# Making the RWKV output gates of a half sequence in one stream of matrix products

## The chip, the cores and the metric

The program runs on one core of one Trainium2 chip. The metric is the time of one execution on the device in microseconds; three executions of the kernel before took 3402.66, 3409.33 and 3413.01 us (median 3409.33). The profiled execution is a fourth one.

## The reference

A two-layer decoder over 1024 positions with 1024 channels, batch 1, all in float32: layer 0 is an RWKV-7 time mixing and a squared-ReLU MLP, layer 1 a forgetting attention on a shared K/V and a second MLP. Each is preceded by an RMS norm with a shift and a scale made from a conditioning vector. The part that the change touches is the output gate `g` of the time mixing:

```python
xr, xw, xk, xv, xa, xg = (h + xx * mu[j] for j in range(6))   # xx: shifted token minus token
r = xr @ wr; k = xk @ wk; v = xv @ wv
g = jax.nn.sigmoid(xg @ g1) @ g2          # g1 (1024, 160), g2 (160, 1024)
y = wkv7_scan(rh, decay, kh, vh, -kk, kk * ah)      # 16 heads of 64, one step a token
y = group_norm(y) * ln_w + ln_b + bonus
return (y * g) @ wo
```

## The kernel before

Everything lies transposed: 128 channels of one of 8 blocks on the partitions, tokens along the free axis. The sequence is cut into two halves of 512 tokens. A large product (`proj`, L150) takes one 128x1024 weight block at a time: SP loads it into `wraw`, ACT rounds it to float32r into `wh` (L116), POOL makes the remainder `wl` (L117), and `mm3` (L120) adds three float32r passes of TensorE into one PSUM bank: wh x hh (L124), wh x hl (L126), wl x hh (L128). The inputs are split in the same way: ACT casts `hh` (L166), DVE subtracts `hl` (L167). `wraw`, `wh` and `wl` have two buffers each. Products on plain float32 operands, as the small ones of the recurrence, take two MATMUL instructions each in the trace.

`phase_rwkv` (L440) makes what layer 0 needs: `stream` (L581) computes r, k and v of a half and stores them in DRAM, its mixed inputs coming from `shift` (POOL, L658) and `mix` (DVE, L663). The conditioning vector's products are made on DVE (`mod`, L182), spread between these. `lora_g` (L564) computes sigmoid(xg @ g1): two float32 products per channel block (L573), one of 128 rows and one of 32, then Tanh on ACT (L577) and a multiply-add on POOL (L578). The 128 rows go to DRAM as `gad` (L579), the 32 stay in partitions 96 to 127 of `zt`.

`phase_wkv` (L667) is the recurrence, in 16 units of two channel blocks by 256 tokens. Units 0 to 7 are the first half, 8 to 15 the second. `early` and `late` prepare a unit, `chain` (L845) runs its four chunks of 64 tokens one after the other, with three steps each, and `gate` (L916) finishes it while the next unit's chain runs: the group norm (L923 to L928), the weights lnw and lnb (L935, L936), then the gate. For this it loads `gad` and the two blocks of g2 (L921, L933, L934), multiplies them with float32 products, 128 rows (L937) and 32 rows (L938) for each of the two channel blocks, and DVE multiplies y with the result in PSUM (L940).

The order is set in two layers. In the program, `units` (L955) gives each step of a chain a ration of `early` and `late`, of the last unit's `gate`, and of dense work from another generator (`beside`): the streams of the second half, then the output product wo and the MLP of the first half. A `yield` in that code is one piece of a ration. In the first half, `rest` (L534) runs `lora_g` beside the end of the r stream, before unit 0. On top of that, the tile framework schedules the instructions of each engine by a simulated timeline, and gives the chain's steps priority. Each engine then runs its own list in order.

## Time and profile before

| | |
|---|---|
| median of three executions | 3409.33 us |
| the profiled execution | 3409.55 us, its span 3407.8 us (1.75 us lie outside) |
| TensorE, matmul busy | 3212.7 us (94% of the span), mean granted clock 0.969 |
| DVE / ACT / POOL busy | 2092.3 / 1431.1 / 1368.4 us (61% / 42% / 40%) |
| start and end of the gates | first gate product at 394.71 us, last one at 1313.83 us |

A matmul's busy time is from its start to its modelled end, and neighbours overlap in the pipeline, so what a product costs TensorE is read from the start of one to the start of the next. "Idle before" is the time in which an engine had nothing running ahead of an instruction, with the instruction that ended the wait. The span divides for this change into the preparation of the first half (up to about 330 us), the 16 units (330 to 1320 us), and the rest, in which the layer's second half, the MLPs and the attention follow.

### The profile page before, as it was taken

How to read it: one execution, taken by the hardware profiler on the slowest of the kernel's cores; microseconds unless marked ns; L12 is line 12 of the kernel's file. 1: busy time of each engine (PE TensorE's matmuls, PEld its weight loads, DVE VectorE, ACT ScalarE, POOL GpSimd, SP SyncE). 2: the span in 40 equal slices, each digit the busy share in tenths (PEclk: the TensorE clock that was granted, in tenths of full speed). 3: DMA queues.
4: the chain of work that ended last, by engine and by line, in shares of the span. 5: the costliest groups of instructions: out<-in, count | busy, mean ns of one | idle time of the engine just before them, and what ended most of it. 6: DMA issues, size and time to landing. Idle time of an engine off the chain costs nothing. (4 is left out here: it accounts for less than half of the span.)

```text
span 3407.8 us, 50293 instructions
## 1 busy us (share of the span) xinstructions
PE 3212.7 (94%) x19108; PEld 2441.4 (72%) x19108; DVE 2092.3 (61%) x3239; ACT 1431.1 (42%) x2284; POOL 1368.4 (40%) x868
## 2 busy tenths in 40 slices
PE   4798999999999998899999999999999999999997
PEld 2466666666777776678878777777778888778886
DVE  7496765666656546377795433555577776455555
ACT  3632236433423223242242556667555454332323
POOL 3464333333433333454434432444433333554444
PEclk7899999899999999999999999999999999999999
DMA  7365344354333225345542233666544442232322
GB/s 270 104 231 154 94 123 139 119 151 143 100 91 106 88 75 177 124 130 173 184 137 95 82 134 115 208 200 182 174 128 138 143 134 95 91 105 99 99 96 84
DMA packets 294064, 452.88 MB, mean 133 GB/s; under 512 B 114720, under 2 KB 170432, under 8 KB 293824
## 3 DMA queue, kind: packets, MB, share of 16 engines
q1 hardware_dynamic: 293824, 449.68, 42.2%
q8 instruction: 151, 2.47, 0.3%
q14 instruction: 89, 0.73, 0.1%
HBM read 371.25 MB, written 78.32 MB: 132 GB/s over the span
## 5 line engine op out<-in xcount | busy, mean ns | idle before, releaser
L117 POOL TENSOR_TENSOR wl<-wraw,wh 128x1024 fp32r<-128x1024 f32 x385 | 951.4, 2472 | 1221.8 <-ACT wh L116 1164.2
L116 ACT CAST wh<-wraw 128x1024 fp32r<-128x1024 f32 x385 | 402.6, 1046 | 709.8 <-PE pk L126 298.2
L124 PE MATMUL pj<-hh,wh 128*128 128x512 f32 x1120 | 449.8, 409 | 9.2 <-ACT wh L116 2.2
L128 PE MATMUL pj<-hh,wl 128*128 128x512 f32 x1120 | 443.2, 401 | 6.0 <-POOL wl L117 6.0
L126 PE MATMUL pj<-hl,wh 128*128 128x512 f32 x1120 | 442.3, 400 | 0.0
L1040 DVE TENSOR_TENSOR mr<-mr 128x512 f32<-128x512 f32 x128 | 276.7, 2163 | 221.5 <-ACT mr L1039 221.3
L1010 DVE SCALAR_TENSOR_TENSOR x<-pj,G,x 128x512 f32<-128x512 f32 x304 | 223.8, 745 | 130.9 <-PE pj L128 129.6
L128 PE MATMUL pk<-hh,wl 128*128 128x512 f32 x688 | 273.5, 404 | 9.7 <-POOL wl L117 9.7
L124 PE MATMUL pk<-hh,wh 128*128 128x512 f32 x688 | 271.5, 400 | 9.7 <-ACT wh L116 6.7
L126 PE MATMUL pk<-hl,wh 128*128 128x512 f32 x688 | 269.4, 398 | 0.0
L124 PEld LDWEIGHTS pj<-hh,wh 128*128 128x128 f32 x1120 | 210.8, 189 | 64.8 <-issue 4.6
L128 PEld LDWEIGHTS pj<-hh,wl 128*128 128x128 f32 x1120 | 210.6, 188 | 59.8 <-POOL wl L117 8.4
L124 PE MATMUL pj<-mh,wh 128*128 128x512 f32 x564 | 237.2, 421 | 17.0 <-DVE x L1010 16.8
L126 PEld LDWEIGHTS pj<-hl,wh 128*128 128x128 f32 x1120 | 210.6, 188 | 47.2 <-issue 2.6
L166 ACT CAST mh<-mr 128x512 fp32r<-128x512 f32 x128 | 79.4, 620 | 372.6 <-DVE mr L1040 206.3
L126 PE MATMUL pj<-ml,wh 128*128 128x512 f32 x564 | 224.4, 398 | 0.0
L1010 DVE SCALAR_TENSOR_TENSOR x<-pk,G,x 128x512 f32<-128x512 f32 x240 | 173.6, 744 | 81.5 <-PE pk L128 81.5
L128 PE MATMUL pj<-mh,wl 128*128 128x512 f32 x564 | 218.6, 399 | 0.0
L182 DVE SCALAR_TENSOR_TENSOR modacc<-modw,cact,modacc 128x1024 f32<-128x1024 f32 x98 | 162.7, 1661 | 39.6 <-DMA modw<-in_modw_dram 26.1
L124 PE MATMUL pk<-mh,wh 128*128 128x512 f32 x460 | 181.4, 396 | 3.5 <-DVE x L1010 3.5
L126 PE MATMUL pk<-ml,wh 128*128 128x512 f32 x460 | 181.3, 394 | 0.0
L128 PE MATMUL pk<-mh,wl 128*128 128x512 f32 x460 | 167.1, 397 | 2.0 <-POOL wl L117 2.0
(333 smaller groups left out, 6502.3 us busy)
## 6 DMA issues: line engine op xcount, KB each, us to landing
wraw<-in_up_dram SPq DMA_DIRECT2D x128, 512.0 KB
wraw<-in_down_dram SPq DMA_DIRECT2D x128, 512.0 KB
modw<-in_modw_dram SPq DMA_DIRECT2D x96, 512.0 KB
wraw<-in_wqg_dram SPq DMA_DIRECT2D x32, 512.0 KB
wraw<-in_wk_dram SPq DMA_DIRECT2D x24, 512.0 KB
wraw<-in_wv_dram SPq DMA_DIRECT2D x24, 512.0 KB
x<-in_xT_dram SPq DMA_DIRECT2D x32, 256.0 KB
wraw<-in_wr_dram SPq DMA_DIRECT2D x16, 512.0 KB
```

The source lines that it names most:

```text
L116: nc.scalar.copy(out=wh, in_=raw)
L117: self.weng.tensor_tensor(out=wl, in0=raw, in1=wh.bitcast(F32), op=ALU.subtract)
L124: mm(out=p, lhsT=wh, rhs=hh[k], start=first, stop=False)
L126: mm(out=p, lhsT=wh, rhs=hl[k], start=False, stop=False)
L128: mm(out=p, lhsT=wl, rhs=hh[k], start=False, stop=last)
L166: self.nc.scalar.copy(out=out_h, in_=src)
L182: nc.vector.scalar_tensor_tensor(out=acc, in0=w, scalar=ck, in1=acc, op0=ALU.mult, op1=ALU.add)
L1010: self.nc.vector.scalar_tensor_tensor(out=x[j][m], in0=ps, scalar=gain[:, m:m + 1], in1=x[j][m], op0=ALU.mult, op1=ALU.add)
L1040: nc.vector.tensor_tensor(out=r, in0=r, in1=r, op=ALU.mult)
```

## The change

`lora_g` now goes on to the gate itself. The 128 rows of sigmoid(xg @ g1) are split into `gh` and `gl`, the 32 last rows into three blocks of one tile `gr`: the rounded rows in partitions 0 to 31 and again in 64 to 95, the remainder in 32 to 63. g2's first 128 rows are loaded as a weight block with `load_w`, its last 32 three times into one block `wr`, whose third copy becomes the remainder. Then, for each of the 8 channel blocks, three passes of `mm3` and one pass with `wr` and `gr` (96 rows) give g; ACT evicts it and SP stores it in DRAM (`gd`). `gate` loads the 128x512 block of g that its unit needs and multiplies it with y on POOL. The bank of `pms` that held the float32 gate products, the loads of g2 and `gad`, and the DVE multiplication go. `gate` has one yield less, `lora_g` eight more.

```diff
--- before.py
+++ after.py
@@ -292,7 +292,7 @@
             self.Fd = dt("Fd", [NH, 2, T])
             self.Ld = dt("Ld", [2 * KT, 128, 8, HD])
             self.T16d = dt("T16d", [2 * KT, 2, 64, 256])
-            self.gad = dt("gad", [128, T])
+            self.gd = dt("gd", [KT, 128, T])
 
             self.tp = self.pool(es, "tmp", 4)
             self.wp = self.pool(es, "wring", 3)
@@ -303,7 +303,7 @@
 
             er = es.enter_context(ExitStack())
             zp = self.pool(er, "zp")
-            self.zt = zp.tile([128, T], F32, name="zt")
+            self.zt = zp.tile([65, T], F32, name="zt")
             self.sv = zp.tile([128, KT, HD], F32, name="sv")
             self.pe = self.pool(er, "pe", space=PSUM)
             el = es.enter_context(ExitStack())
@@ -529,10 +529,10 @@
             yield from self.lora_wa(h, 1, lw, al)
             for i in (1, 2, 0):
                 yield from self.stream(h, 1, i, xj, ev, al)
-            yield from self.lora_g(h, 1, lw)
+            yield from self.lora_g(h, 1, lw, xj, ev)
 
         def rest():
-            for _ in self.both(self.lora_g(h, 0, lw), r, 3):
+            for _ in self.both(self.lora_g(h, 0, lw, xj, ev), r, 3):
                 self.take(m, self.NMD)
                 yield
             self.drain(m)
@@ -561,22 +561,44 @@
         S.activation(out=self.zt[0:64, s], in_=ps[0:64], func=AF.Tanh)
         S.copy(out=al[:, s], in_=ps[64:128])
 
-    def lora_g(self, h, j, lw):
-
-        nc, S = self.nc, self.nc.scalar
+    def lora_g(self, h, j, lw, xj, ev):
+
+
+        nc, S, V, G = self.nc, self.nc.scalar, self.nc.vector, self.nc.gpsimd
         s = slice(j * HT, (j + 1) * HT)
         ps = [self.bank() for _ in range(2)]
         for k in range(KT):
             w = lw(("g1",), k)
             xg = self.mix(h[j][k], self.shift(h[j][k]), 5, k)
-            for p, o, n in ((ps[0], 0, 128), (ps[1][96:128], 128, 32)):
+            for p, o, n in ((ps[0], 0, 128), (ps[1][0:32], 128, 32)):
                 nc.tensor.matmul(out=p, lhsT=w[:, o:o + n], rhs=xg, start=k == 0, stop=k == KT - 1)
                 yield
         g = self.t()
-        for a, p in ((g, ps[0]), (self.zt[96:128, s], ps[1][96:128])):
-            S.activation(out=a, in_=p, func=AF.Tanh, scale=0.5)
-            nc.gpsimd.tensor_scalar(out=a, in0=a, scalar1=0.5, scalar2=0.5, op0=ALU.mult, op1=ALU.add)
-        nc.sync.dma_start(out=self.gad[:, s], in_=g)
+        gh, gl = (xj.tile([128, HT], F32R, name=n, tag=n) for n in ("xh", "xl"))
+        S.activation(out=g, in_=ps[0], func=AF.Tanh, scale=0.5)
+        G.tensor_scalar(out=g, in0=g, scalar1=0.5, scalar2=0.5, op0=ALU.mult, op1=ALU.add)
+        self.split(gh, gl, g)
+        r = self.t()
+        gr = xj.tile([128, HT], F32R, name="xh", tag="xh")
+        S.activation(out=r[0:32], in_=ps[1][0:32], func=AF.Tanh, scale=0.5)
+        G.tensor_scalar(out=r[0:32], in0=r[0:32], scalar1=0.5, scalar2=0.5, op0=ALU.mult, op1=ALU.add)
+        S.copy(out=gr[0:32], in_=r[0:32])
+        S.copy(out=gr[64:96], in_=r[0:32])
+        V.tensor_tensor(out=gr[32:64], in0=r[0:32], in1=gr[0:32].bitcast(F32), op=ALU.subtract)
+        wh, wl = self.load_w(self.ap["g2"][:, 0:128].rearrange("m k n -> k m n"))
+        raw, wr = (self.wp.tile([128, KT, 128], d, name=n, tag=n, bufs=b) for n, d, b in (("wraw", F32, self.NW[0]), ("wh", F32R, self.NW[1])))
+        for i in range(3):
+            nc.sync.dma_start(out=raw[i * 32:(i + 1) * 32], in_=self.ap["g2"][:, 128:160].rearrange("m k n -> k m n"))
+        S.copy(out=wr[0:96], in_=raw[0:96])
+        self.weng.tensor_tensor(out=wr[64:96], in0=raw[64:96], in1=wr[64:96].bitcast(F32), op=ALU.subtract)
+        for m in range(KT):
+            p = self.bank()
+            self.mm3([p], wh[:, m], wl[:, m], [(j, [gh], [gl])], 0, True, False)
+            nc.tensor.matmul(out=p, lhsT=wr[0:96, m], rhs=gr[0:96], start=False, stop=True)
+            yield
+            o = ev.tile([128, HT], F32, name="e0", tag="e0")
+            S.copy(out=o, in_=p)
+            nc.sync.dma_start(out=self.gd[m][:, s], in_=o)
 
     def stream(self, h, half, which, xj, ev, al, lead=2):
 
@@ -917,8 +939,8 @@
 
             j, p, ts = where(u)
             y, bv, rs = w["y"], self.t(), self.t()
-            ga = lng("ga", [128, 256], 1)
-            nc.sync.dma_start(out=ga, in_=self.gad[:, ts])
+            g = lng("g", [128, W], 1)
+            nc.sync.dma_start(out=two(g), in_=pair(self.gd, p, ts))
             nc.sync.dma_start(out=two(bv), in_=pair(self.bvd, p, ts))
             S.activation(out=rs, in_=y, func=AF.Square)
             ps = self.small()
@@ -926,18 +948,12 @@
             yield
             S.activation(out=rs, in_=ps, func=AF.Ln, bias=self.gneps)
             S.activation(out=rs, in_=rs, func=AF.Exp, scale=-0.5)
-            ps = self.small()
             for q in range(2):
                 c = slice(q * 256, (q + 1) * 256)
-                g2 = lng("g2", [128, 2, 128], 1)
-                nc.sync.dma_start(out=g2[:, 0], in_=ap["g2"][p + q][0:128])
-                nc.sync.dma_start(out=g2[96:128, 1], in_=ap["g2"][p + q][128:160])
                 V.scalar_tensor_tensor(out=y[:, c], in0=y[:, c], scalar=self.col("lnw", p + q), in1=rs[:, c], op0=ALU.mult, op1=ALU.mult)
                 V.scalar_tensor_tensor(out=y[:, c], in0=y[:, c], scalar=self.col("lnb", p + q), in1=bv[:, c], op0=ALU.add, op1=ALU.add)
-                PE.matmul(out=ps[:, c], lhsT=g2[:, 0], rhs=ga, start=True, stop=False)
-                PE.matmul(out=ps[:, c], lhsT=g2[96:128, 1], rhs=self.zt[96:128, ts], start=False, stop=True)
-                yield
-            V.tensor_tensor(out=y, in0=y, in1=ps, op=ALU.mult)
+            yield
+            G.tensor_tensor(out=y, in0=y, in1=g, op=ALU.mult)
             nc.sync.dma_start(out=pair(self.yd, p, ts), in_=two(y))
             self.ngated += 1
```

The order moves at these three places. In the rows below the names before and after the arrow are the tiles written and read; numbers tell buffers apart.

TensorE at the end of the first half's r stream (`wh_1688` is the last block of wr). Before, the v stream (`wh_1800`) follows:

```order
L124 MATMUL pk_1693<-xh_1050,wh_1688 128x512
L126 MATMUL pk_1693<-xl_1051,wh_1688 128x512
L128 MATMUL pk_1693<-xh_1050,wl_1689 128x512
L124 MATMUL pj_1811<-xh_1739,wh_1800 128x512
L126 MATMUL pj_1811<-xl_1740,wh_1800 128x512
L128 MATMUL pj_1811<-xh_1739,wl_1801 128x512
```

In the changed kernel (`wh_1744` is g2, `wh_1885` the first block of wv; left out between the two pieces are 26 rows of gate passes, one row of small products of `mod` and eight of `late`):

```order
L128 MATMUL pk_1693<-xh_1050,wl_1689 128x512
L124 MATMUL pk_1756<-xh_1730,wh_1744 128x512
L124 MATMUL pj_1764<-xh_1730,wh_1744 128x512
L124 MATMUL pj_1772<-xh_1730,wh_1744 128x512
L124 MATMUL pk_1780<-xh_1730,wh_1744 128x512
L126 MATMUL pk_1756<-xl_1731,wh_1744 128x512
L128 MATMUL pk_1756<-xh_1730,wl_1745 128x512
```

```order
L124 MATMUL pj_1896<-xh_1824,wh_1885 128x512
L126 MATMUL pj_1896<-xl_1825,wh_1885 128x512
L128 MATMUL pj_1896<-xh_1824,wl_1886 128x512
```

The 32 gate passes of the first half stand between the r and the v stream, and `wh_1885` and the block after it can be cast only when the buffers of `wh_1744` and of `wr` are free.

TensorE in the gate of unit 1, before (`g2_3532` is a block of g2, `zt` holds the 32 rows, `pl` belongs to `late`, `pj` to a stream):

```order
L793 MATMUL pl_3648<-ar_2954,bk_2955 128x128
L937 MATMUL pms_3531<-ga_3501,g2_3532 128x256
L938 MATMUL pms_3531<-zt_123,g2_3532 128x256
L793 MATMUL pl_3649<-ar_2954,bk_2955 128x128
L124 MATMUL pj_3454<-xh_2833,wh_3449 128x512
```

In the changed kernel, after the same unit's group-norm product (`blk_m`), only the stream, the chain and `late` are left:

```order
L947 MATMUL pms_3579<-t_3574,blk_m_68 128x512
L124 MATMUL pj_3528<-xh_2894,wh_3523 128x512
L126 MATMUL pj_3528<-xl_2895,wh_3523 128x512
L128 MATMUL pj_3528<-xh_2894,wl_3524 128x512
L124 MATMUL pj_3528<-xh_2902,wh_3523 128x512
```

The two products of each channel block are gone from the list, and nothing stands in their place.

POOL around the gate of unit 1, before (`sp` is the chain's decayed state, `wl` a weight remainder):

```order
L734 TENSOR_SCALAR sg_3495<-sg_3495 128x512
L739 COPY pc_3515<-P_1135 128x8
L861 TENSOR_TENSOR sp_3550<-st_3543,pc_2393 128x128
L117 TENSOR_TENSOR wl_3842<-wraw_3840,wh_3841 128x1024
L861 TENSOR_TENSOR sp_3734<-st_3727,pc_2393 128x128
```

And in the changed kernel:

```order
L756 TENSOR_SCALAR sg_3569<-sg_3569 128x512
L761 COPY pc_3589<-P_1135 128x8
L956 TENSOR_TENSOR y_3549<-y_3549,g_3575 128x512
L883 TENSOR_TENSOR sp_3620<-st_3613,pc_2478 128x128
L117 TENSOR_TENSOR wl_3905<-wraw_3903,wh_3904 128x1024
L883 TENSOR_TENSOR sp_3797<-st_3790,pc_2478 128x128
```

The multiplication with g stands ahead of a decayed state and of a weight remainder, and these wait behind it.

## Rows read from the trace of the kernel before

**Rows 1.** Stretches: start:end, length, busy us of PE, PEld, DVE, ACT, POOL; clock; DMA.

```profile
330.00:1320.00 990.00, 962.63 (x8694) 676.38 (x8694) 607.97 (x1286) 367.69 (x571) 343.98 (x271) 0.98 0.39 113
254.00:286.00 32.00, 21.49 (x80) 14.72 (x80) 30.95 (x39) 8.01 (x12) 20.16 (x14) 0.79 0.44 144
```

**Rows 2.** Waits of PE in 330 to 1320 us: total us, times, longest.

```profile
PE pj L126 <- DVE xl L167: 8.3, 4, 4.5
PE pj L124 <- DVE x L1010: 6.5, 6, 2.0
PE pq L869 <- DVE st L904: 4.3, 2, 3.3
PE pq L900 <- DVE uv L893: 1.9, 3, 0.8
PE py L909 <- ACT uv L892: 1.5, 3, 0.8
```

**Rows 3.** PE in order of time, the first and the last gate: start, us, what.

```profile
394.71 0.70 PE L937 MATMUL pms<-ga,g 128*128 128x256 f32 x2
395.34 0.69 PE L938 MATMUL pms<-zt,g 32*128 32x256 f32 x2
...
1309.17 0.59 PE L937 MATMUL pms<-ga,g 128*128 128x256 f32 x2
1309.69 0.69 PE L938 MATMUL pms<-zt,g 32*128 32x256 f32 x2
1310.31 0.50 PE L124 MATMUL pj<-mh,wh 128*128 128x512 f32 x1
1310.65 0.40 PE L126 MATMUL pj<-ml,wh 128*128 128x512 f32 x1
1310.88 0.40 PE L128 MATMUL pj<-mh,wl 128*128 128x512 f32 x1
```

**Rows 4.** Groups of instructions in 330 to 1320 us: busy us, mean ns, idle before.

```profile
L938 PE MATMUL pms<-zt,g 32*128 32x256 f32 x64 | 22.4, 429 | 0.0
L937 PE MATMUL pms<-ga,g 128*128 128x256 f32 x64 | 21.5, 418 | 0.0
L940 DVE TENSOR_TENSOR y<-y,pms 128x512 f32<-128x512 f32 x16 | 11.0, 685 | 7.5 <-PE pms L938 7.4
```

**Rows 5.** PE in order of time, the first half's r and v streams.

```profile
239.79 0.63 PE L124 MATMUL pk<-xh,wh 128*128 128x512 f32 x1
240.22 0.63 PE L126 MATMUL pk<-xl,wh 128*128 128x512 f32 x1
...
259.50 0.50 PE L124 MATMUL pj<-xh,wh 128*128 128x512 f32 x1 [2.15 <-ACT xh L166]
...
266.06 0.79 PE L126 MATMUL pj<-xl,wh 128*128 128x512 f32 x1 [2.63 <-DVE xl L167]
```

**Rows 6.** ACT in order of time, behind the first half's Tanh.

```profile
246.24 1.05 ACT L116 CAST wh<-wraw 128x1024 fp32r<-128x1024 f32 x1 [8.40 <-POOL t L578]
```

**Rows 7.** The whole span's POOL products of two SBUF tiles of this size.

```profile
L751 POOL TENSOR_TENSOR bk<-bk,sg 128x512 f32<-128x512 f32 x16 | 21.0, 1310 | 31.2 <-DVE sg L750 31.2
L1350 POOL TENSOR_TENSOR rb<-rb,g 128x512 f32<-128x512 f32 x16 | 20.6, 1288 | 44.2 <-DMA rb<-rd 44.2
```

**Rows 8.** POOL, DVE and PE in order of time around the gate at 943 us.

```profile
943.98 0.48 DVE L935 SCALAR_TENSOR_TENSOR y<-y,prm,t 128x256 f32<-128x256 f32 x1
...
944.90 2.38 POOL L117 TENSOR_TENSOR wl<-wraw,wh 128x1024 fp32r<-128x1024 f32 x1 [1.45 <-ACT wh L116]
...
945.30 2.27 DVE L935 SCALAR_TENSOR_TENSOR y<-y,prm,t 128x256 f32<-128x256 f32 x1
...
948.80 0.50 PE L124 MATMUL pj<-mh,wh 128*128 128x512 f32 x1 [1.98 <-DVE x L1010]
```

**Rows 9.** Waits of POOL in 330 to 1320 us: total us, times, longest.

```profile
POOL wl L117 <- ACT wh L116: 285.0, 66, 9.7
POOL sp L861 <- DVE st L904: 122.1, 30, 9.7
```

## The prediction

> **What bounds the kernel now.** I read the stretches first, because the change touches two stages with different limits. In the units, from 330 to 1320 us, TensorE is busy for 962.63 of 990 us at a granted clock of 0.98, while DVE has 607.97, ACT 367.69 and POOL 343.98 us of work [rows 1]. Then the waits of TensorE in that stretch: of the 27.4 us left, the five longest kinds make 22.5 us in 18 waits [rows 2]. So the units are bound by TensorE's list of work: under 3% of the stretch is waiting, and the rest is products one behind the other. A product taken out there shortens the stage, unless what stands behind it isn't ready.
>
> Just before, from 254 to 286 us, it is the other way round: DVE is busy for 30.95 of 32 us, TensorE for 21.49, at a clock of 0.79 [rows 1]. That is where the v stream starts, and TensorE waits there for split inputs, 2.15 us for `xh` and 2.63 us for `xl` in the two longest [rows 5]. Work added there lies beside DVE's list, at least in part.
>
> **What goes.** Each unit has two channel blocks with two float32 products, 64 products in all; each is two instructions in the trace (a row says x2), so that L937 and L938 count 64 instructions each for their 32 products [rows 3, 4]. The starts give the price: in the last gate L937 starts at 1309.17, L938 at 1309.69, the next product at 1310.31, so 0.52 and 0.62 us; in the first gate L937 starts at 394.71 and L938 at 395.34, 0.63 us [rows 3]. Between 0.52 and 0.63 I take 0.61: 64 x 0.61 = 39.0 us. The first pass behind such a group takes 0.34 us (1310.31 to 1310.65) where the next takes 0.23 (1310.65 to 1310.88) [rows 3]; 0.1 us at one such place a unit, 1.6 us. Together -40.6 us, all of it in the TensorE-bound stage. The busy times of the two groups, 22.4 and 21.5 us [rows 4], say nearly the same from above.
>
> The DVE multiplication also goes, 16 x 0.685 = 11.0 us [rows 4], from an engine with 382 us free in the stretch. SP issues five loads a unit fewer and one more, and per half three or four more weight loads and eight stores instead of one; the long waits of TensorE name no transfer [rows 2], so I cost this at nothing. If a block of g came late, only POOL's list would stand behind it, which is the rival below.
>
> **What comes, second half.** 8 blocks x 4 passes of 128x512. A pass in a full row of passes costs 0.23 us (1310.65 to 1310.88) [rows 3]; 32 x 0.234 = 7.5 us, and, since small float32 products stand between the blocks, another 0.1 us at each of 8 changes: +8.3 us. This lies in the units, on the bound. The evictions, casts and stores run on ACT and SP, of which ACT has 62% free [rows 1].
>
> **What comes, first half.** The same 32 passes stand in TensorE's list between r and v. Bounds: nothing, if they fill the time in which TensorE waits for DVE anyway (10.5 us free between 254 and 286 us [rows 1]); less than nothing is out, since nothing starts earlier by them. From above, every pass at the slower level of the clock, 1.2 GHz, which shows there as 0.43 us from start to start (239.79 to 240.22) [rows 5]: 32 x 0.43 = 13.7 us; and the wait for the gates' input. In the run before, POOL took up the Tanh of this stream so late that ACT's next cast waited 8.4 us [rows 6], and this POOL step now stands ahead of the split that the passes need. 13.7 + 8.4 = 22 us. I take 5 us, near the lower end: the row that decides is DVE's 30.95 of 32 us. The v stream is paced by its own splits, and DVE gets only two subtractions more (0.7 us and a fraction of it), while POOL gets two weight remainders of 2.4 us each, which can hold DVE up as shown next.
>
> **POOL's multiplication.** POOL takes about 1.29 us for a product of this size (1288 and 1310 ns [rows 7]), 16 x 1.29 = 20.6 us on an engine with 646 us free. Its price is what it does to others. At 944.90 us POOL starts a weight remainder of 2.38 us; DVE's L935, which takes 0.48 us before it, takes 2.27 us beside it, and TensorE then waits 1.98 us for DVE [rows 8]. So a POOL operation can stop a DVE operation for its whole length. The Trainium skill, page "SBUF — State Buffer", section "SBUF: two separate sides", has this as a rule: DVE and GpSimd share one pair of ports under an exclusive lock, also for a DVE operation with two SBUF inputs against a GpSimd operation that reads SBUF, and the loser is blocked for the whole instruction; the trace agrees (2.27 against 0.48 us). By that rule alone the move of the multiplication would be a loss on DVE, 20.6 us of lock for 11.0 us of work taken off. On the end it counts only where TensorE waits for DVE: four kinds of waits for DVE make 21.0 us in a stretch in which POOL was busy for 344 us [rows 1, 2], an upper share of 0.06 us per us of POOL. 20.6 x 0.06 = +1.3 us; bounds 0 and 20.6.
>
> **Cover that is lost.** The removed products also gave the chain time. TensorE waits at the 18 places of [rows 2], while the units have 16 x 12 = 192 chain steps, so about one step in ten is late already; if time taken out turns into waiting at the same rate, 40.6 / 10 = +4 us. Bounds: 0, and all 40.6, if every gate's products stood in front of something late.
>
> **Sum.** -40.6 + 8.3 + 5 + 1.3 + 4 = -22.0 us. Against the profiled execution, 3409.55 us (0.2 us over the median), that is 3387.5 us. Behind the units the same products remain, with four yields of the MLP moved there; I count nothing for it.
>
> **Rivals.**
> First, the chain is what paces the units, and TensorE's list only fills them. Then the 40.6 us turn into waits, and the second half's 8.3 us too; the first half's 5 us and POOL's 1.3 stay: 3416 us at worst, 3410 if the units keep their time to the us. For it: ACT's and DVE's waits for the chain's products are many. Against it: TensorE waited only 7.7 us in all for the chain's `st`, `uv` [rows 2], 0.5 us a unit against the 2.5 us a unit that go.
>
> Second, the first half's stream lies on the path in full, at 22 us: 3409.55 - 40.6 + 8.3 + 22 + 5.3 = 3404.6 us, about no change. For it: the v stream's first two weight blocks can't be cast before the stream is done with both buffers. Against it: DVE paces this stretch.
>
> Third, on the slower side: POOL works its list in order, and the multiplication waits there for DVE's lnb step and for the load of g. Behind it stand a decayed state, which the chain needs, and a weight remainder, which the stream needs. POOL's waits for `st` reach 9.7 us [rows 9]; a wait of 3 us a unit on top of 1.29, passed on to TensorE, gives 16 x 4.3 = 69 us instead of 1.3: 3387.5 + 68 = 3455 us. It decides from about 1.4 us passed on in each unit (22 / 16). Against it: the state is asked for first by DVE, and weight remainders are made a block ahead; TensorE's longest waits hold none for POOL [rows 2]. The Trainium skill, page "TensorE: Matmul & The Clock Gate", section "Architectural detail: the array is 16× 32×32, not 1× 128×128", calls GpSimd's queue a strict first-in first-out one; in the trace POOL does sit idle for 285 us before weight remainders [rows 9], though no row shows one overtaken.
>
> **How the numbers follow.** The forecast has 0.72, the first rival 0.10, the second 0.10, the third 0.08. The forecast's own range is 3377 (no cost but the second half's passes: 3409.55 - 40.6 + 8.3) to 3400 (the first half near 14 us and a cover loss of 8). For 8 in 10 the range reaches over the second rival and part of the first, and down a little below the full gain, since the new order can also close waits: 3373 to 3409. A measurement of this kernel tells about 0.3%, 10.2 us, from no change. Faster by more: 0.68 of the forecast and a little of the second rival, 0.70. Within: the two rivals and the forecast's edge, 0.20. Slower: the third and the worst of the first, 0.10.
>
> **What would show it.** In the changed profile the 128 instructions of the gate are gone and 64 passes of 0.23 to 0.24 us are there; the last gate ends some 20 us earlier, and the units are still above 95% TensorE. The time from the end of the r stream to the first chain step tells the first half's term. Wrong would be: TensorE's waits in the units well above 40 us, named for `st` or `uv` (first rival) or `wl` and `sp` (third), or the first unit starting 20 us later (second).

## The result, and the profile after

Four executions of the changed kernel took 3443.47 to 3451.23 us, median 3450.61, beside 3409.14 for the kernel before: a ratio of 1.0122, 95% interval [1.0104, 1.0140]. The forecast was 3387.5 us, with 3409 as the upper end. The change is 41 us slower, not 22 us faster.

The profiled execution of after, the fastest of its four, took 3443.47 us, 33.9 more than that of before; the sums below account for these 33.9 us. I divide the span first by the ends of the chains: each chain ends with a copy of its result on ACT, and the start of that copy is the mark. These are the first and the last such copy, of before and of after (start, us, what):

```profile
378.56 0.58 ACT L912 COPY y<-py 128x512 f32<-128x512 f32 x1
...
1301.53 0.59 ACT L912 COPY y<-py 128x512 f32<-128x512 f32 x1 [0.87 <-PE py L909]
```

```profile
398.46 0.59 ACT L934 COPY y<-py 128x512 f32<-128x512 f32 x1 [1.45 <-PE py L931]
...
1306.69 0.58 ACT L934 COPY y<-py 128x512 f32<-128x512 f32 x1
```

So chain 0 ends 19.9 us late, the 15 units behind it win 14.7 us back, and 28.7 us are lost behind the last chain, where the products are the same but for the last gate's and six yields of the MLP that moved there. The same division, with chain 7 as a third mark, for every kernel of this study (profiled executions, us; "behind" is the span less the end of chain 15; medians and ratios from the timed runs, each ratio to executions of before in the same batch, whose medians lie between 3405.99 and 3409.14, so that it is not the quotient of two cells of this table):

| kernel | chain 0 ends | 0 to 7 | 7 to 15 | behind | median | ratio to before |
|---|---|---|---|---|---|---|
| before | 378.6 | 377.9 | 545.0 | 2106.3 | 3409.14 | 1 |
| after | 398.5 | 373.3 | 534.9 | 2135.0 | 3450.61 | 1.0122 [1.0104, 1.0140] |
| a_realign | 395.9 | 380.1 | 540.2 | 2112.5 | 3430.19 | 1.0078 [1.0061, 1.0094] |
| half1 | 377.6 | 378.0 | 534.3 | 2110.9 | 3405.94 | 1.0006 [0.9996, 1.0016] |
| half0 | 397.1 | 379.8 | 556.2 | 2108.0 | 3442.89 | 1.0112 [1.0095, 1.0129] |
| g0late | 382.3 | 384.4 | 553.6 | 2081.7 | 3404.72 | 1.0001 [0.9992, 1.0010] |
| b_rot | 379.2 | 377.0 | 546.0 | 2119.5 | 3424.89 | 1.0045 [1.0028, 1.0061] |
| b_cut0 | 376.6 | 378.6 | 559.9 | 2108.3 | 3420.41 | 1.0032 [1.0020, 1.0045] |
| b_cut1 | 379.2 | 381.6 | 540.5 | 2113.8 | 3411.73 | 1.0010 [0.9997, 1.0022] |
| a_na | 396.7 | 385.1 | 536.4 | 2082.8 | 3402.29 | 0.9984 [0.9969, 0.9998] |
| a_1pass | 406.9 | 370.7 | 537.7 | 2106.0 | 3428.03 | 1.0060 [1.0043, 1.0076] |
| a_noev | 388.4 | 372.6 | 538.2 | 2108.8 | 3409.02 | 1.0005 [0.9994, 1.0017] |
| a_vmul_r | 396.8 | 375.8 | 541.9 | 2108.3 | 3424.62 | 1.0048 [1.0034, 1.0063] |
| half1_nd | 379.3 | 379.1 | 534.9 | 2082.6 | 3378.93 | 0.9915 [0.9900, 0.9930] |
| b_nd | 376.9 | 378.3 | 545.8 | 2068.3 | 3374.38 | 0.9899 [0.9883, 0.9915] |
| a_nd | 397.2 | 371.1 | 535.3 | 2084.1 | 3393.55 | 0.9962 [0.9947, 0.9977] |
| b_nd_na | 381.0 | 393.9 | 550.0 | 2073.3 | 3400.05 | 0.9984 [0.9973, 0.9995] |
| h1_nd_na | 381.6 | 398.4 | 548.2 | 2076.3 | 3412.39 | 1.0020 [1.0010, 1.0030] |
| g0_nd_na | 383.8 | 395.1 | 557.7 | 2082.8 | 3413.91 | 1.0032 [1.0020, 1.0045] |

How far to trust one cell: after, a_realign and a_nd have the same list on TensorE up to the last gate, and their stretches from 0 to 7 took 373.3, 380.1 and 371.1 us, at granted clocks of 0.95, 0.92 and 0.96. So one stretch of one execution is good to some 9 us, the clock too differs between executions of one list, and differences that several kernels repeat are better than that. The end of chain 0 repeats best: 395.9 to 398.5 us in the six kernels with the whole stream of the first half ahead of it (after, a_realign, half0, a_na, a_vmul_r, a_nd).

Up to the end of chain 15, that list of after took 1306.7, 1316.2 and 1303.6 us, and the list of before 1301.5, 1302.2 (b_rot) and 1300.9 (b_nd). There the change costs some 7 us in the mean of three executions each; the rest of the loss lies behind the last chain.

**The units.** This is what [rows 1] have become (columns as there). The first fence shows before, by the two stretches between the marks; the second shows after, by the stretches of [rows 1] and then by the same marks:

```profile
378.60:756.50 377.90, 364.68 (x3653) 254.14 (x3654) 236.63 (x581) 169.81 (x265) 127.36 (x114) 0.95 0.43 126
756.50:1301.50 545.00, 534.35 (x4483) 381.65 (x4483) 318.09 (x621) 179.04 (x277) 185.44 (x132) 0.99 0.35 103
```

```profile
330.00:1320.00 990.00, 951.89 (x8759) 673.70 (x8759) 606.34 (x1278) 380.39 (x591) 377.65 (x290) 0.97 0.39 118
254.00:286.00 32.00, 20.14 (x83) 15.21 (x82) 31.83 (x38) 13.49 (x22) 25.90 (x16) 0.71 0.53 175
...
398.50:771.80 373.30, 348.42 (x3604) 247.07 (x3604) 237.05 (x565) 172.24 (x266) 134.47 (x122) 0.95 0.43 126
771.80:1306.70 534.90, 526.61 (x4432) 376.12 (x4433) 314.33 (x612) 184.90 (x288) 206.54 (x142) 0.99 0.37 112
```

Between the ends of chains 0 and 7, TensorE lost 16.3 us of busy time, and 11.7 us of that came back as idle time (13.2 before, 24.9 after): 4.6 us are won. The longest waits of TensorE in after, which answer to [rows 2] (total, times, longest), are for the chain's `uv` and `st`, 15.4 us in these three kinds for 7.7 before; in before the stream's waits came first:

```profile
PE pq L922 <- DVE uv L915: 6.1, 5, 2.4
PE pq L891 <- DVE st L926: 5.0, 4, 2.4
PE py L931 <- ACT uv L914: 4.3, 7, 1.6
```

**The first half's start.** TensorE there, with its waits (answers to [rows 5]), and ACT beside it:

```profile
264.05 0.80 PE L597 MATMUL pk<-xh,wh 96*128 96x512 f32 x1 [4.08 <-POOL wh L593]
267.86 0.80 PE L124 MATMUL pk<-xh,wh 128*128 128x512 f32 x1 [1.30 <-ACT e L600]
279.10 2.08 PE L815 MATMUL pl<-ar,bk 64*128 64x128 f32 x16 [4.96 <-ACT e L600]
282.70 0.80 PE L124 MATMUL pj<-xh,wh 128*128 128x512 f32 x1 [1.52 <-ACT e L600]
```

```profile
266.70 0.62 ACT L166 CAST xh<-t 128x512 fp32r<-128x512 f32 x1 [5.69 <-DVE t L685]
267.22 0.58 ACT L600 COPY e<-pk 128x512 f32<-128x512 f32 x1
...
281.54 0.62 ACT L166 CAST xh<-t 128x512 fp32r<-128x512 f32 x1 [2.50 <-DVE t L685]
282.06 0.58 ACT L600 COPY e<-pj 128x512 f32<-128x512 f32 x1
285.29 0.59 ACT L600 COPY e<-pj 128x512 f32<-128x512 f32 x1 [2.65 <-DMA gd<-e]
```

First the passes wait 4.08 us for POOL's remainder of the stacked weights (L593). Then the evictions of the gates (L600) stand in ACT's list between the casts for the v stream (L166), and these wait for DVE, which is busy for 31.83 of 32 us; the last eviction also waits 2.65 us for a store. So a bank of the gates comes free at the pace of DVE's list, and TensorE waits for it: at 279.10 for the scores of the first unit, at 282.70 for the v stream, whose first pass stood at 253.64 us before. ACT's wait of 8.40 us for POOL in [rows 6], the smaller part of the upper bound of 22, became waits of 0.85 and 2.90 us behind the Tanh.

**Behind the units.** TensorE's waits in the MLP's end and the K/V projections, first before (1985 to 2580 us), then after (1997 to 2612 us, the same products):

```profile
PE pms L1129 <- ACT sq L1126: 3.0, 1, 3.0
PE ps L1280 <- DMA qa<-Qhd: 2.2, 1, 2.2
PE ps L1279 <- ACT P L1290: 2.2, 1, 2.2
...
PE pj L128 <- POOL wl L117: 2.0, 2, 1.8
```

```profile
PE pmt L1145 <- DVE sq L206: 6.0, 2, 5.5
PE ps L1295 <- ACT P L1306: 5.7, 5, 2.4
PE pj L124 <- ACT sq L1117: 5.1, 3, 4.0
PE pk L128 <- POOL wl L117: 4.2, 4, 1.3
```

The stretch took 595 us before and 615 after: 20 of the 28.7 us. Nothing in the diff stands here. Of the rest, 6.8 us lie between the last chain and this stretch (683.5 and 690.3 us), where the six yields of the MLP have moved to: 18 passes in TensorE's list, 4.2 us at 0.234 each.

### The profile page after: what moved, and what is told of

It reads as the page before. It is cut to its first block, busy times and chain, and to the rows that moved or that the text cites. A ratio compares the mean times of both kernels' runs of the same rounds, so it can differ in the third digit from the quotient of the medians.

```text
span 3441.7 us, 50146 instructions
## 1 busy us (share of the span) xinstructions
PE 3204.0 (93%) x19044; PEld 2436.2 (71%) x19044; DVE 2102.6 (61%) x3227; ACT 1447.8 (42%) x2308; POOL 1401.8 (41%) x888
## 4 chain that ended last, share of the span: by engine, by line
PE 46%; DVE 6%; ACT 3%; DMA 1%; issue 1%; POOL 1%; DVEq 0%; ACTq 0%; SPq 0%; POOLq 0%
PE pj L124 7%; PE pj L126 7%; PE pj L128 7%; PE pk L128 6%; PE pk L124 6%; PE pk L126 6%; PE pt L1338 2%; PE po L1324 1%; PE po L1323 1%; PE ps L1295 1%; PE ps L1296 1%; POOL wl L117 1%; DVE t L236 1%; DMA modw<-in_kvmodw_dram 1%; DVE hl L238 1%
## 5 line engine op out<-in xcount | busy, mean ns | idle before, releaser
L124 PE MATMUL pj<-hh,wh 128*128 128x512 f32 x1096 | 448.0, 411 | 14.7 <-ACT sq L1117 5.1
L126 PE MATMUL pj<-hl,wh 128*128 128x512 f32 x1096 | 441.6, 403 | 1.6 <-DVE hl L238 1.6
L128 PE MATMUL pk<-hh,wl 128*128 128x512 f32 (+1 forms) x712 | 275.8, 402 | 16.1 <-POOL wl L117 16.1
L124 PE MATMUL pk<-hh,wh 128*128 128x512 f32 (+1 forms) x712 | 274.4, 399 | 8.4 <-ACT wh L116 7.1
L126 PE MATMUL pk<-hl,wh 128*128 128x512 f32 (+1 forms) x712 | 273.1, 397 | 0.0
L126 PEld LDWEIGHTS pj<-hl,wh 128*128 128x128 f32 x1096 | 209.0, 191 | 49.3 <-issue 4.1
L126 PE MATMUL pj<-ml,wh 128*128 128x512 f32 x568 | 225.8, 397 | 0.0
L166 ACT CAST mh<-mr 128x512 fp32r<-128x512 f32 x128 | 79.4, 620 | 323.9 <-DVE mr L1056 210.0
L124 PE MATMUL pk<-mh,wh 128*128 128x512 f32 x456 | 181.2, 399 | 15.8 <-DVE x L1026 15.8
L182 DVE SCALAR_TENSOR_TENSOR modacc<-modw,cact,modacc 128x1024 f32<-128x1024 f32 x98 | 161.8, 1651 | 31.5 <-DMA modw<-in_modw_dram 18.4
L126 PE MATMUL pk<-ml,wh 128*128 128x512 f32 x456 | 180.4, 396 | 0.0
L128 PEld LDWEIGHTS pk<-hh,wl 128*128 128x128 f32 (+1 forms) x712 | 133.4, 188 | 54.4 <-POOL wl L117 22.8
```

The costliest lines, as they stand in the source:

```text
L124: mm(out=p, lhsT=wh, rhs=hh[k], start=first, stop=False)
L126: mm(out=p, lhsT=wh, rhs=hl[k], start=False, stop=False)
L128: mm(out=p, lhsT=wl, rhs=hh[k], start=False, stop=last)
L166: self.nc.scalar.copy(out=out_h, in_=src)
L182: nc.vector.scalar_tensor_tensor(out=acc, in0=w, scalar=ck, in1=acc, op0=ALU.mult, op1=ALU.add)
```

## The experiments

**1. The rotation of the banks.** `bank` takes the accumulators in turn from a list, by a counter that runs through the program; behind the units the list has 6 places. The stream takes 16 banks, and 16 is not a multiple of 6. Two runs: after with the counter set right, and before with the counter set wrong.

```diff
 # a_realign: end of lora_g
+        self.nbank += 2 * j
 # b_rot: end of lora_g in the kernel before
+        self.nbank += 4 * j
```

> The changed kernel with one number added: the counter that picks the accumulator banks is raised by 2 behind the second half's gate stream, so that with its 16 new banks it has moved by 18, a multiple of the 6 places of the list, and the products behind the units take the same pj and pk banks as in the kernel before. No work is added or removed. Theory A (the 32 us lost behind the units come from the shifted rotation, which made the scheduler choose another order there): 3450.6 - 32 = about 3418, and the lag behind the kernel before stays near +2 us from 1320 us to the end. Rival B (they come from the four yields of the first half's MLP that slipped behind the units, or from anything else in the units): 3445 to 3451, and the lag grows after 1320 us as before. If the rotation does half of it: 3434.

> The kernel before with its bank counter raised by 4 behind the second half's gates, the shift that the changed kernel's 16 new banks cause; no work is changed. Theory A (the shift reshuffles the scheduler's order behind the units and costs 20 us, what the realignment gave back): 3420 to 3432. Rival (the shift alone is harmless, and the changed kernel lost only together with its other position in the MLP): 3403 to 3409.

a_realign won 20.4 us of median, all of it behind the units (2135.0 to 2112.5), b_rot lost 18.4 to the executions of before beside it; by the ratios, 0.0044 and 0.0045, both are 15 us. The work is the same in each pair, and so is TensorE's list up to the last gate; behind it the scheduler has made another list. In the stretch shown above the wrong counter has the waits of after, the right one those of before. b_rot (1975 to 2594 us), then a_realign (2008 to 2602 us), the window's row and the first waits:

```profile
1975.00:2594.00 619.00, 578.23 (x2850) 456.18 (x2849) 331.16 (x560) 370.04 (x675) 231.66 (x182) 0.97 0.51 158
...
PE ps L1280 <- ACT P L1291: 6.9, 6, 2.3
PE pmt L1130 <- DVE sq L206: 6.0, 2, 5.5
PE pj L124 <- ACT sq L1102: 4.6, 2, 4.0
PE pk L128 <- POOL wl L117: 4.2, 4, 1.3
```

```profile
2008.00:2602.00 594.00, 571.74 (x2869) 455.43 (x2868) 319.60 (x559) 368.71 (x675) 232.98 (x181) 0.99 0.53 164
...
PE pms L1146 <- ACT sq L1143: 3.0, 1, 3.0
PE ps L1296 <- ACT P L1307: 2.5, 2, 2.2
PE pj L124 <- DVE sq L1101: 2.3, 2, 1.6
```

619 and 615 us with the shift, 595 and 594 without. In b_rot the order won 10.7 us between the last chain and this stretch, so its cell "behind" is only 13.2 us above that of before. Theory A holds in kind, though less than the 32 us that it priced came back: a third of the loss by the ratios, half by the medians, is an order that the shift alone brings about.

**2. One half at a time.** half1 has the stream in the second half alone, half0 in the first alone, and g0late has all of it, with the first half's passes moved behind the first half's v projection. In all three the counter is set right.

```diff
 # half1 (half0: j == 1): the other half's gates as in the kernel before
+        if j == 0:
+            ...
+            nc.sync.dma_start(out=self.gad[:, s], in_=g)
+            return
 # g0late: dense()
             yield from v
+            yield from self.lora_g2(0, self.g0, None, xj, ev)
```

> Only the second half's gates are made by the dense stream; the first half keeps its two float32 products in each of units 0 to 7. The bank counter is realigned behind the units as in a_realign. Theory C (the first half's stream stands on the path to the first chain and costs 20 us there): chain 0 ends near 379 us as in the kernel before, and the time is the kernel before's plus the second half's own balance, half of the -18 us that the units gained, made worse by its stream: -20.3 for 32 products, +8.3 for the stream, +7 for half of the 14 us that the units lost against the sum, so -5: 3404. Rival D (the multiplication on POOL and the longer stream in the units are what costs, the first half nothing): half of the changed kernel's loss of 41 us stays, 3430, with chain 0 near 398 us. Both suppose that the realigned banks give back the loss behind the units; if they don't, 3436 and 3446.

> The opposite half: only the first half's gates are made by the stream, ahead of the units; units 8 to 15 keep their float32 products. Bank counter realigned. Theory C: chain 0 ends near 398 us (+20), units 0 to 7 save 20.3 us for 32 products less 7 of lost cover, no stream beside the chains: +20 - 13 = +7: 3416. Rival D: as half1, near 3430, with the loss spread over the units. Without the realignment's effect, 32 us more.

> The changed kernel, bank counter realigned, with the first half's four passes by eight moved from ahead of the units into the dense stream beside them, directly behind the first half's v projection; until then the first half's gates wait in two rows of SBUF (the 32 stacked rows where they lay in the kernel before). Theory C: chain 0 ends near 379 us again, and the 32 passes cost 8.3 us beside the chains: units -18 + 8.3 = -10: 3399, below the kernel before. Rival D: the first half's place does not matter, and the time is that of a_realign within 3 us. Rival E (the chain's start is late for another cause than the passes, such as the extra rows and stores on the queues ahead of it): chain 0 ends at 390 us or later, and the time is 3410 or more.

half1 is the kernel before to within 0.2%, half0 is 1.1% slower. The steps from before to after are then by medians 0 (second half, half1), 24 (first half as well, a_realign less half1) and 20 (rotation): 44.7 from half1 to after. Chain 0 is late exactly where the first half's passes stand ahead of it (395.9, 397.1) and not in half1 (377.6) or g0late (382.3). That much of theory C holds, and half1 came out at its 3404 to within 2 us. g0late's time says little about the price: it equals before only by its 2081.7 us behind the units, 24.6 less than before (part 6 has the reason); from chain 0 to 15 it took 15.1 us more. Theory C's price for half0 (3416) failed: the 7 gates taken out of the stretch from chain 0 to 7 won nothing (379.8 for 377.9), and the second half, whose gates are the old ones there, took 556.2 for 545.0; the reason for that stays open.

**3. The products alone.** Before, with the 32 products of one half left out and nothing in their place. Their loads go too, and y is multiplied by another tile.

```diff
 # b_cut0: j == 0, b_cut1: j == 1 (the lines on the loads and on y are left out here)
-                PE.matmul(out=ps[:, c], lhsT=g2[:, 0], rhs=ga, start=True, stop=False)
-                PE.matmul(out=ps[:, c], lhsT=g2[96:128, 1], rhs=self.zt[96:128, ts], start=False, stop=True)
```

> The kernel before with the 32 float32 gate products (and their loads) of units 0 to 7 left out; y is multiplied by another tile there, so the gate itself is missing in the first half. Nothing takes their place. The prediction's step (the units are bound by TensorE, each product 0.61 us): 3406 - 20 = 3386. Rival P (the first half's units are paced by the chain's waits, since the stream beside them is let out at 2.2 yields a step; time taken off TensorE turns into idle and a lower granted clock): 3401 to 3408, with PE's idle from the end of chain 0 to the end of chain 7 some 10 us larger than in the kernel before.

> The same with units 8 to 15, where the stream beside the chains is let out at 3 and then 5.4 yields a step: the 32 products of the second half left out, nothing in their place. The prediction's step: 3386. Rival P says the same here, since TensorE has work in reserve in these units: 3384 to 3390. If the products are hidden in this half too: 3401 to 3408.

Neither is faster: +0.32% and +0.10%, where the prediction's price is -20 us each. Both times lie above every range of their expectations (3408 is the highest end), so the rivals there were too low as well. These are the runs that decide against the prediction's first step. b_cut0 from chain 0 to 7 and from 7 to 15:

```profile
376.60:755.20 378.60, 356.12 (x3603) 253.89 (x3602) 246.46 (x582) 170.76 (x267) 123.40 (x114) 0.93 0.41 119
755.20:1315.10 559.90, 541.10 (x4469) 385.04 (x4470) 327.05 (x620) 177.79 (x277) 184.19 (x133) 0.98 0.34 100
```

Between chains 0 and 7, 7 x 4 x 0.61 = 17.1 us of products are gone; busy time fell by 8.6 us (364.68 to 356.12), idle time rose by 9.3, and the stretch kept its length. The idle time repeats: at the old rate, TensorE is idle there for 13 to 19 us in the six kernels with the old gates in the first half, and for 22 to 28 us in the eight without them.

What b_cut0 lost against before lies from chain 7 to 15, where all its products are left: 559.9 us for 545.0. TensorE's list is not that of before with 32 products missing; the scheduler has made another one, which differs until some 1000 us, so a part of the +0.32% can be the order. In b_cut1 the stretch that lost its products became 4.5 us shorter, and the two others took 3.7 and 7.5 us more, which one execution can't tell from no change. So the products are worth little; that they are worth less than nothing is not shown.

One place shows how idle time and a lower clock come together, b_cut0 by stretches of 4 us and two instructions of the chain in the second of them:

```profile
476.00:480.00 4.00, 4.00 (x22) 2.49 (x20) 1.22 (x1) 3.88 (x5) 0.62 (x2) 1.00 0.67 145
480.00:484.00 4.00, 2.54 (x30) 1.89 (x30) 3.27 (x7) 1.79 (x4) 0.19 (x1) 0.99 0.19 19
484.00:488.00 4.00, 4.00 (x33) 2.79 (x33) 1.07 (x3) 1.53 (x2) 1.96 (x1) 0.50 0.51 146
...
500.00:504.00 4.00, 4.00 (x27) 2.80 (x25) 4.00 (x6) 1.49 (x3) 2.48 (x2) 0.50 0.00 0
504.00:508.00 4.00, 4.00 (x20) 2.92 (x20) 2.98 (x6) 0.54 (x2) 1.86 (x3) 0.95 0.01 4
```

```profile
481.32 0.33 PE L909 MATMUL py<-sc,uv 128*64 128x64 f32 x2 [0.47 <-ACT uv L892]
482.63 0.34 PE L900 MATMUL pq<-uv,bkt 128*64 128x64 f32 x4 [0.99 <-DVE uv L893]
```

TensorE waits 1.46 us for the chain's `uv`. Then it is busy without a gap for 20 us, all of them at a granted clock of 0.50, which is the 1.2 GHz level: about 10 us of work lost behind 1.46 us of idle. In before an idle of 1.33 us (492 to 496 us) left the clock at 1.00, so not each such wait does it, and that this one did is argued from the order of time alone. Nor is it shown how much of the clock of 0.93 in this stretch is due to the products left out, since one list gave 0.92 to 0.96. The Trainium skill, page "TensorE: Matmul & The Clock Gate", section "A second HAM failure mode: psum-queue depth-cycling", tells of a kernel in which short idles between groups of matmuls come often enough that the clock swings between the two levels; this trace has the swing (0.99, then 0.50), but behind one pair of idles, not frequent ones.

**4. POOL's multiplication.** a_realign with y times g on VectorE:

```diff
-            G.tensor_tensor(out=y, in0=y, in1=g, op=ALU.mult)
+            V.tensor_tensor(out=y, in0=y, in1=g, op=ALU.mult)
```

> The realigned changed kernel with the multiplication of y by the gate on VectorE in place of POOL, in all 16 units. If the multiplication on POOL (2.4 us where it runs beside VectorE, by the prediction worth 1.3 us in sum, by its third rival up to 4.3 us a unit in lost cover) is what ate the units' gain: 3430 - 20 or more = 3410 or less. If it is off the path: 3425 to 3434.

3424.62 for 3430.19: 5.6 us by the medians, 0.0030 of the ratio (10 us), with intervals that overlap. So a gain of some 6 to 10 us, at the edge of what the intervals can tell, and not the 20 of the first expectation; the second one's range, 3425 to 3434, is missed by 0.4 us. In after the group reads (busy, mean ns, idle before)

```profile
L956 POOL TENSOR_TENSOR y<-y,g 128x512 f32<-128x512 f32 x16 | 22.1, 1379 | 46.2 <-DVE y L954 38.8 <-DMA lblk<-Ld 5.7 <-PE pq L922 1.7
```

which is [rows 7] with 1379 for 1310 ns; a single one took 1.26 to 1.72 us, never the 2.4 us that the expectation has. The waits in this row are POOL's, for DVE's y above all, and no wait of TensorE from 330 to 1320 us in after is put down to POOL.

**5. What makes chain 0 late.** a_realign with 8 of the first half's 32 passes, and with none of them, no evictions and no stores (its units of the first half then multiply y by other rows of DRAM).

```diff
 # a_1pass, first half
-            self.mm3([p], wh[:, m], wl[:, m], [(j, [gh], [gl])], 0, True, False)
-            nc.tensor.matmul(out=p, lhsT=wr[0:96, m], rhs=gr[0:96], start=False, stop=True)
+            nc.tensor.matmul(out=p, lhsT=wh[:, m], rhs=gh, start=True, stop=True)
 # a_noev (the line that loads other rows is left out here)
-        for m in range(KT):
+        for m in range(KT if j else 0):
```

> The realigned changed kernel (3430) with three of the four passes of each accumulator left out in the first half's gate stream: 8 passes in place of 32 ahead of the units. The weights' loads, casts and differences, the 8 evictions and the 8 stores all stay. The first half's gates are then only the leading product. Theory S1 (the first chain is late because TensorE has 32 more passes, at 0.43 us each, ahead of the v projection): 24 x 0.43 = 10 us come back, chain 0 ends near 386 us, and the time is near 3420. Theory S2 (it is late because of what surrounds the passes: the accumulator banks that wait for ScalarE's evictions and the two-tile ring of their stores, and POOL's 2.7 us difference of the stacked weights): chain 0 still ends at 394 to 398 us, and the time stays within 3426 to 3434.

> The realigned changed kernel (3430) with the first half's passes, evictions and stores left out altogether, while its weights are still loaded, cast and subtracted and its gates still split into three stream tiles; the units of the first half then multiply y by other rows of DRAM, so the first half's gate is missing. Theory S2 (what follows the passes holds the first chain up: banks and tiles waiting in ScalarE's queue behind casts that wait for VectorE, and the stores): chain 0 ends at 376 to 383 us, as in the kernel before, and the time is near 3410. Theory S3 (what goes ahead of the passes does: the extra splits, differences and casts on VectorE, POOL and ScalarE, in a stretch in which VectorE is 99% busy, and the three tiles taken from the ring of the v projection's operands): chain 0 still ends at 390 us or later, and the time stays near 3428. A share of each: 384 to 390.

Theory S1 fell: with a quarter of the passes chain 0 ends at 406.9 us, 11 us later than with all. So the time of TensorE's passes is not the price. Without passes, evictions and stores it ends at 388.4, so 10 us belong to the preparation of weights and gates, beside a DVE that has no time there, and the rest of the 17 us to passes, evictions, banks and stores together; that it is the evictions and banks is argued from a_1pass and from the waits for them. Both theories had a part. With 8 passes the evictions wait in the same way, at other places of ACT's list, and TensorE waits longer for them: 3.21, 5.28 and 7.76 us, for 1.55, 4.88 and 1.54 in a_realign. That is 8 of the 11 us; why the places are worse stays open.

**6. A wait behind the units, in all kernels so far.** Just behind the last chain, the o projection of the second half waits in the kernel before for its weights. TensorE and ACT in before:

```profile
1370.73 0.50 PE L124 MATMUL pk<-hh,wh 128*128 128x512 f32 x1 [0.95 <-ACT wh L116]
1373.40 0.79 PE L128 MATMUL pk<-hh,wl 128*128 128x512 f32 x1 [1.93 <-POOL wl L117]
```

```profile
1369.63 1.04 ACT L116 CAST wh<-wraw 128x1024 fp32r<-128x1024 f32 x1 [9.33 <-PE pk L126]
...
1379.92 1.04 ACT L116 CAST wh<-wraw 128x1024 fp32r<-128x1024 f32 x1 [4.17 <-PE pk L126]
```

Each cast starts when the last L126 of the block in work has run, so no block is prepared ahead: of two buffers one serves. The other would be held by an MLP block that the program has begun and not finished. a_na, made for part 7, had lost the wait; half1_nd and b_nd test it with the pair of numbers that says how many yields of the MLP go ahead of the projection.

```diff
-    ND = (20, 40)
+    ND = (36, 24)      # half1_nd, a_nd;  (30, 30) in b_nd
```

> The realigned changed kernel (3430) with the stream beside units 0 to 6 let out at 2.4 yields a step in place of 2.2, some 14 to 16 yields or 45 passes more there. Rival P (the first half's units are paced, and idle TensorE time there can be filled with passes that the chains don't wait for): the units take hardly longer and 45 passes of 0.23 us are gone later, so 3430 - 8 to 10 = 3421. The prediction's step (TensorE is the bound in these units): the passes only change places, 3428 to 3432.

> The kernel with the stream in the second half alone (half1, 3406), with one pair of numbers changed: 36 and 24 yields of the first half's MLP, in place of 20 and 40, are let out ahead of and behind the second half's o projection. Theory H (where these yields end inside a group of the down products, its weight tile stays held through the whole o projection, whose own weights then have one of the ring's two tiles left: waits for wh and wl of some 12 us, and TensorE at the lower clock, in 84 us): 36 yields end inside a group of the up products, the waits for wl between 1300 and 1400 us fall from 8.7 to under 3 us, and the time falls by 15 to 22 us: 3384 to 3391. Rival: the waits stay, as the weights come late for another reason: 3402 to 3409.

> The control to half1_nd: the kernel before with 30 and 30 yields in place of 20 and 40, which also ends inside a group of the up products. No work is changed. Theory H: 3406 - 15 to 22 = 3384 to 3391, the same gain without any change to the gates. If half1_nd is faster and this one is not, the gain belongs to the second half's stream. If neither is, theory H falls.

> The realigned changed kernel (3430) with 36 and 24 yields of the MLP around the second half's o projection, as in half1_nd: both things that move the order behind the units are then as good as in b_nd (3374), and what is left between the two is what the change costs up to the last gate. If the wait behind the units and the late first chain are separate and add up: 3430 - 30 = 3400, 24 to 27 us above b_nd, the same distance as between a_realign and half1. If the late units shield the second half's o projection from its wait: 3410 or more.

a_na is 28 us faster than a_realign, but not for the reason in its expectation: its units are not shorter, the 30 us are behind them. b_nd is the fastest kernel of the study, 0.9899 of before, with no change to any computation. It and half1_nd won more than the 15 to 22 us expected (34 and 29 by the ratios). From 1316 to 1400 us, before, then b_nd:

```profile
1316.00:1400.00 84.00, 66.98 (x248) 51.02 (x247) 45.85 (x42) 19.50 (x28) 27.61 (x13) 0.88 0.63 212
```

```profile
1316.00:1400.00 84.00, 84.00 (x371) 68.21 (x370) 52.68 (x51) 27.11 (x38) 48.09 (x21) 1.00 0.71 242
```

Nearly all of b_nd's gain lies here: a row of TensorE's list that stands at 1325.3 us in before stands at 1324.6 in b_nd, and one 300 rows later at 1424.9 and 1392.0.

By the program's count, and in TensorE's lists, the yields end inside a group of the down products in the eleven kernels that took 2106 to 2135 us behind the last chain, and inside a group of the up products, or at a group's end, in the eight that took 2068 to 2084. So theory H is borne out by all 19; that it is the held buffer is argued from the casts. With both orders set right, a_nd stands 0.0063 of ratio (21 us) above b_nd, and half1_nd 0.0016 (5 us, with intervals that overlap). But up to the end of chain 15 a_nd is only 2.6 us later than b_nd, and half1_nd 7.7 us earlier; 15.8 and 14.3 us lie behind it, where the rations are (36, 24) for (30, 30). So what the change itself would cost or give with the same order behind the units is not shown.

**7. A faster stream.** If the chains leave TensorE idle, a higher rate could fill it.

```diff
-    NA = 2.2
+    NA = 2.4      # in a_na, b_nd_na, h1_nd_na (ND 30, 30) and g0_nd_na (g0late, ND 30, 30)
```

> All gates by the stream, both halves' passes beside the chains (g0late), with the stream let out at 2.4 yields a step, which makes room for its 16 yields, and with the MLP stopped inside a group of the up products as in half1_nd and b_nd. If TensorE time saved in the units can be turned into time once the pace of the stream is raised with it: b_nd's 3374 less 25 (40.6 for the products, 16.6 for the stream): 3350. If the units are held by the chains and the clock, as b_cut0 says: 3370 to 3382, no better than b_nd.

> half1_nd (3379) with the stream beside units 0 to 6 let out at 2.4 yields a step and 30 and 30 yields of the MLP around the o projection. If a faster stream fills what the chains leave idle: 3379 - 6 = 3373 or less. If not: 3377 to 3385.

> The control: the kernel before with 30 and 30 yields around the o projection (b_nd, 3374) and 2.4 yields a step. Its stream then reaches the MLP earlier and waits there for the eighth gate, so some 14 yields bring nothing: 3372 to 3380. If it gains as much as the two kernels with the new gates, their gain is the pace and not the gates.

It doesn't. The three kernels with both numbers changed came out 20 to 32 us above the highest end of their ranges, and b_nd_na is 26 us slower than b_nd. With the higher rate the stretch from chain 0 to 7 takes 385 to 398 us in all four. What the rate brought into it in b_nd_na is not more three-pass work (555 passes for 561 in b_nd) but 21 instructions of the second half's float32 products with g1 (L573), 10.6 us of busy time; the stretch grew by 15.6 us, and those behind it did not shrink (550.0 for 545.8, 2073.3 for 2068.3). So work added there cost its time or more; why it was not won back later stays open.

## Why the prediction was wrong

**Products, -40.6 us.** The step that failed first: "A product taken out there shortens the stage". The condition that the prediction adds, "unless what stands behind it isn't ready", is what came about, and the sum had it at 4 us. Left out alone, the products of a half brought no time (b_cut0, b_cut1), where 20 us each were priced. At the old rate the stretch from 0 to 7 takes 371 to 380 us with the first half's stream ahead of it (mean of seven 374.8) and 377 to 382 with the old gates (six, 378.7); from 7 to 15 it takes 534 to 542 with the second half's stream (eight, 537.2; g0late, 553.6, falls out), and 545 or 546 in before, b_rot and b_nd. So some 4 and 8 us are won, of 32.5 by the prediction's prices: 15 gates x 4 x 0.61 = 36.6 in the two stretches, less 8.3 for the stream, plus 4.2 for the six yields of the MLP (18 passes of 0.234 in TensorE's lists, where the prediction had four yields) that moved behind the units. TensorE's 97% was read as a list of work. It was work that hid the chain's waits: take it out, and they show. From chain 0 to 7 this is shown by the idle time, 22 to 28 us for 13 to 19; what the clock adds is not settled, and from 7 to 15 the idle time did not grow in after (10.7 us before, 8.3 after). The first rival said this. Its sign, waits well above 40 us, was set too high: TensorE's idle time from 330 to 1320 us is 38.1 us (990 - 951.89), since the lower clock takes its share as busy time.

**Lost cover, +4 us.** The term for just that, between 0 and 40.6. It took the share of steps that were late already. The right value is some 20 us (12 won of 32.5), five times the term. The first rival, which let all of it be lost, has a slip: its 3410 leaves out the 5 us that it keeps for the first half's stream.

**First half's stream, +5 us.** Measured 17 to 20 us at the end of chain 0, near the upper bound of 22 and the second rival. That the size fits is luck: the bound was added up from 13.7 us of slow passes and a wait of 8.4 us for POOL, and a quarter of the passes brought chain 0 no earlier, while that wait became 0.85 and 2.90 us. The lower end was chosen because DVE is full there and TensorE has idle time. The same row says the opposite for everything that the stream needs besides TensorE: its splits, differences and evictions stand in lists paced by DVE.

**Second half's stream, +8.3 us.** Not contradicted: half1 won 10.7 us from 7 to 15, where 17.1 - 8.3 + 4.2 = 13.0 were due. No run measured it by itself.

**POOL, +1.3 us, and the third rival.** The term was small, and what was measured for it, some 6 to 10 us, is at the edge of the noise. The third rival's time, 3455, came close to the result by luck; its 69 us by way of POOL are not there.

**Behind the units, nothing.** 28.7 us, of which 15 to 20 by the rotation, which stood in no rival. This is the second step that failed, a term put at nothing: the prediction knew that the same products remain; that a scheduler decides their order from all that stands ahead of it, the counter of banks too, was left out.

None of these alone makes the result. In the profiled execution it is 3409.55 + 19.9 - 14.7 + 28.7 = 3443.5: nearly the second rival's price for the first half's stream, less than half of the 32.5 us due in the units, and an order behind the units that nobody had priced.

## What to carry to other kernels

A busy share of 97% does not say what a removed instruction is worth; leave it out alone, and time that, before building its replacement, and look whether the scheduler has made another list of what is left. Work put ahead of a long chain is priced by the fullest engine there, and by the in-order lists that its evictions join, not by the idle time of the engine that does the products. Where a scheduler sets the order, compare a change only with its counters, rotations and rations set to the same places as before: here an empty shift cost 0.45% and another ration gave 1%, nearly as much as the change itself cost.

## What was not expected of the hardware

An idle of 1.46 us on TensorE was followed by 20 us at a granted clock of 0.50, with no further gap in them, while an idle of 1.33 us in another run was followed by full clock. And three executions with the same list on TensorE differ by 9 us in a stretch of 380 us, at granted clocks of 0.92, 0.95 and 0.96.
